# Two feature blocks of a feed-forward layer in ordinary products, on negated token quarters

## The chip, the cores and the metric

The kernel runs on one core of a Trainium2 chip. The metric is the time of the execution on the device in microseconds, the median of several runs: 866.68 us before the change.

## What is computed

One decoder layer on 544 tokens (512 prompt tokens and 32 sample tokens), of width 1024. A token mixer with three branches and an output projection comes first, then a layer norm, a SwiGLU feed-forward part with 2816 inner features, and a second layer norm. Only the seam between the first norm and the feed-forward part matters here:

```python
xp = _layernorm(ALPHA * xp + mp, ln1_g[l], ln1_b[l])
xp = _layernorm(ALPHA * xp + _ffn(xp, ffn_w_gate[l], ffn_w_up[l], ffn_w_down[l]), ln2_g[l], ln2_b[l])
...
def _ffn(x, wg, wu, wd):
    return (jax.nn.silu(x @ wg) * (x @ wu)) @ wd
```

## The kernel before

All matrix products are float32 products made of three passes: each operand is split into a high and a low part in float32r (`hi_lo`: ScalarE copies the high part, VectorE subtracts it to get the low part), and `gemm` (line 220) issues for every 128 rows of the contraction the matmuls high by high, high by low, low by high. Line 228 is the matmul of nearly all of them.

**The seam.** The output projection (`proj`) makes eight slices of 128 channels for two token halves, 288 and 256 tokens. ScalarE copies each result out of PSUM (`mo`, line 867), TensorE transposes it to tokens (line 819), VectorE adds the residual (line 878). `normalize` forms the norm, and `features` transposes the rows back (line 896) and writes the normalised tensor `xf` by channels with ScalarE (line 897). `xf` is 8 slices of 128 channels by 544 tokens.

**The feed-forward part.** The 2816 features are 22 blocks of 128, taken in two chunks of 11 (`NFC`). For a block, gate and up are one product of a 2x2 matrix of weight quarters (gate and up by two halves of the 1024 channels) with a 2x2 matrix of token quarters: `A11`, `A12` are the two channel halves of the first 272 tokens (`TH`), `A21`, `A22` those of the other 272. The kernel makes it with seven products in place of eight (Strassen's scheme in Winograd's form): `do(1, f)` to `do(7, f)`, each 12 matmuls of 272 columns. Their token operands `S[1]` to `S[7]` are made once: `S[1]` is -A11, `S[2]` is A12, `S[4]` is -A22, and 5, 6, 3, 7 are differences of quarters (`less`, line 1028) in the tiles `s1` to `s4` of the pool `sx`. Each is split by `operand` in two halves of its four channel slices. The weight operands are made per block: `prep_gate(f)` splits the two gate quarters, which serve products 1 and 2, and `prep_sums(f)` forms sums of the quarters and splits them for products 5, 7, 6, 3 and 4. Raw weights come with `ffn_load` into two buffers (`rawp`); split weights stand in a ring of three buffers (`wp`, tag `w`, shared with the projection's weights), one of two (`wpe`, tag `e`) and one of two (`t4`). The gate's and up's results are multiplied into `g`, which `put_g` splits into `gh` (ScalarE, line 977) and `gl` (GpSimd, line 978), the operands of the down projection.

Work is written in program order; a scheduler (the framework's own timeline) orders the instructions of each engine, and each engine then runs its queue in that order. At the seam the program writes:

```python
        operand(1, A11, True)
        operand(2, A12)
        do(1, 0)
        do(2, 0)
        prep_gate(1)
        do(1, 1)
        do(2, 1)
        less(s1, A21, A22)
        operand(5, s1)
        prep_sums(0)
```

so four products (48 matmuls) need only A11 and A12, and the fifth needs a difference of quarters, its split, and the sums of block 0's weights.

Of the kernel before, what the change touches and what calls it, by code (L numbers as in the profile page):

```python
# [16 lines left out]
P = 128  # L17
# [42 lines left out]
CNU = 0  # L60
KRB = 6
NFC = NF // 2
TH = T // 2
PSM = 5
W0C = ((0, 4), (4, 8))
# [83 lines left out]
def hybrid_layer_kernel(  # L149
# [747 lines left out]
            nc.scalar.activation(xf[:, kt, c0:c1], tp[:, :c1 - c0], AF.Identity, bias=vcol(V_B1 + kt), scale=vcol(V_G1 + kt))  # L897


    raws, gops, tops = {}, {}, {}  # L900

    def ffn_load(f):
        r = rawp.tile([P, 2048], F32, tag="raw", name=f"rawf{f}").rearrange("p (a c) -> p a c", a=4)
# [11 lines left out]
    def blocks(t, a):  # L915
        return [x[:, 512 * a:512 * a + 512].rearrange("p (k c) -> p k c", c=P) for x in t]

    def prep_gate(f):
        t = pair_of(wp, "w", 1024)
        hi_lo(t[0], t[1], raws[f][:, 0:2].rearrange("p a c -> p (a c)"))  # L920
        gops[f] = (blocks(t, 0), blocks(t, 1))

    def prep_sums(f):
        r = raws[f]
# [19 lines left out]
    ffn_load(0)  # L944
    ffn_load(1)
    prep_gate(0)
    for m in range(4):
        proj(res[m], 4 + m, 0)
    normalize(0)
    kts = iter(range(KD))  # L950
    for m in range(4):
        proj(res[m], 4 + m, 1)
        features(0, [next(kts) for _ in range(FEAT[m])])
    normalize(1)
    features(0, kts)
    features(1, range(KD))
# [23 lines left out]
    def do(i, f):  # L980
        if i == 1:
            X[f] = bank()
            prod(X[f], 1, f, True)
            M[f] = tmp("m", 2)
            nc.scalar.copy(M[f], X[f][:, :TH])
        elif i == 5:
            Y[f] = bank()
            prod(Y[f], 5, f, True)
            Q5[f] = tmp("q5", 2)
            nc.scalar.copy(Q5[f], Y[f][:, :TH])  # L990
        elif i == 2:
            Z[f] = bank()
            prod(Z[f], 2, f, True)
            SG1[f] = tmp("sg1", 2)
            nc.vector.tensor_tensor(out=SG1[f], in0=Z[f][:, :TH], in1=M[f], op=ALU.subtract)
            lasts.append(nc.scalar.activation(SG1[f], SG1[f], AF.Silu))
        elif i == 6:
            prod(X[f], 6, f, False)
            U2[f] = tmp("u2")
            nc.scalar.copy(U2[f], X[f][:, :TH])  # L1000
        elif i == 3:
            prod(Y[f], 3, f, False)
            g = tmp("g1")
            nc.vector.tensor_tensor(out=g, in0=Y[f][:, :TH], in1=U2[f], op=ALU.add)
            nc.vector.tensor_tensor(out=g, in0=g, in1=SG1[f], op=ALU.mult)
            put_g(g, f, 0)
        elif i == 7:
            prod(X[f], 7, f, False)
            C22[f] = tmp("c22")
            nc.vector.tensor_tensor(out=C22[f], in0=X[f][:, :TH], in1=Q5[f], op=ALU.add)  # L1010
        else:
            prod(X[f], 4, f, False)
            g = tmp("sg2")
            lasts.append(nc.scalar.activation(g, X[f][:, :TH], AF.Silu, scale=-1.0))
            nc.vector.tensor_tensor(out=g, in0=g, in1=C22[f], op=ALU.mult)
            put_g(g, f, TH)

    def operand(i, src, neg=False):
        h, l = S[i]
        for k in (slice(0, 2), slice(2, 4)):  # L1020
            if neg:
                nc.scalar.mul(h[:, k], src[:, k], -1.0)
                nc.vector.scalar_tensor_tensor(out=l[:, k], in0=src[:, k], scalar=-1.0, in1=h[:, k].bitcast(F32), op0=ALU.mult, op1=ALU.subtract)
            else:
                hi_lo(h[:, k], l[:, k], src[:, k])

    def less(out, a, b):
        nc.vector.tensor_tensor(out=out, in0=a, in1=b, op=ALU.subtract)

    with pool("sx", side="right", reuse_waits="tile") as sx:  # L1030
        s1, s2, s3, s4 = (sx.tile([P, 4, TH], F32, name=f"sx{i}") for i in range(4))
        operand(1, A11, True)
        operand(2, A12)
        do(1, 0)
        do(2, 0)
        prep_gate(1)
        do(1, 1)
        do(2, 1)
        less(s1, A21, A22)
        operand(5, s1)  # L1040
        prep_sums(0)
        less(s2, A11, s1)
        operand(6, s2)
        less(s4, A12, s2)
        operand(3, s4)
        less(s3, A21, A11)
        operand(7, s3)
        operand(4, A22, True)
    gp = ctx.enter_context(pool("gp", side="right", reuse_waits="tile"))
    gh = gp.tile([P, NFC, T], F32R, name="gh")  # L1050
    gl = gp.tile([P, NFC, T], F32R, name="gl")
    G = (gh, gl)
    pieces = ((0, 6), (6, 5))
    wds = []
# [6 lines left out]

    def ffn_blocks(f0, f1, todo):
        for f in range(f0, f1):
            if f + 2 < f1 and f + 2 > 1:
                ffn_load(f + 2)
            if f + 1 < f1:
                if f + 1 not in gops:
                    prep_gate(f + 1)
            else:
                todo()  # L1070
            for i in (6, 3):
                do(i, f)
            if f + 1 < f1:
                prep_sums(f + 1)
            do(7, f)
            if f + 1 < f1:
                do(1, f + 1)
            do(4, f)
            if f + 1 < f1:
                do(5, f + 1)  # L1080
                do(2, f + 1)

    for i in (5, 6, 3, 7, 4):
        do(i, 0)
    prep_sums(1)
    do(5, 1)

    def warm(wd):
        wd.prepare(0)
        wd.prepare(1)  # L1090

    ffn_load(2)
    ffn_blocks(1, NFC, lambda: warm(wds[0]))
    for m in range(KD):
        pss = [bank(), bank()]
        for j, (k0, k) in enumerate(pieces):
# [193 lines left out]
```

## Time and profile before

| | us |
|---|---|
| Three runs | 865.34, 866.68, 867.08 |
| Median | 866.68 |
| The profiled execution | 872.77 |
| Its span | 871.0 |
| TensorE busy in it | 827.4 (95%) |
| TensorE weight loads busy | 779.1 (89%) |
| VectorE busy | 580.5 (67%) |
| ScalarE busy | 413.4 (47%) |
| GpSimd busy | 174.1 (20%) |

The profile is of one execution. TensorE is busy in nearly all of the span; where it isn't, or where its granted clock is half, the stretch has to be looked at by itself. The page cuts the span into 40 slices of 21.8 us; the slice with the lowest granted clock begins at 479 us. A row's bracket gives the idle time of the engine before it and what ended it.

### The profile page before, as it was taken

The page shows a single profiled execution, that of the slowest core. Times are in us where ns is not written, and L with a number is a line of the kernel's source. Part 1 is how long each engine was busy: PE and PEld are TensorE (multiplying, and loading weights), DVE is VectorE, ACT ScalarE, POOL GpSimd, SP SyncE. Part 2 cuts the span into 40 slices and gives each one's busy share as a digit, 9 for nine tenths or more (in the row PEclk, how much of TensorE's full clock was granted, in tenths as well). Part 3 has the DMA queues.
Part 4 walks back from the last instruction along what each step waited for, and adds up shares of the span by engine and source line. Part 5 has one row for each costly group of instructions (what it writes and reads, how often), then busy time and mean ns, then how long its engine had stood idle before and what let it go on. Part 6 is the DMA issues. An engine that isn't in the chain of part 4 may idle for free.

```text
span 871.0 us, 16214 instructions
## 1 busy us (share of the span) xinstructions
PE 827.4 (95%) x6683; PEld 779.1 (89%) x6683; DVE 580.5 (67%) x968; ACT 413.4 (47%) x711; POOL 174.1 (20%) x198
## 2 busy tenths in 40 slices
PE   8998899999999998999998699999999999999992
PEld 7998799888898786789997699999999999999992
DVE  4899956888555544469455999883337888843436
ACT  5334368677654324344316556553124555543231
POOL 1430000002547766210000032211000111110002
PEclk9999899999999998999999699999999999999997
DMA  9413132412738987673500153322225333312222
GB/s 297 125 48 106 55 93 62 147 40 87 266 119 289 341 320 259 216 272 116 146 2 1 48 145 99 97 68 82 85 83 146 98 98 100 108 55 83 74 93 103
DMA packets 119401, 110.35 MB, mean 127 GB/s; under 512 B 4896, under 2 KB 111232, under 8 KB 117152
## 3 DMA queue, kind: packets, MB, share of 16 engines
q1 hardware_dynamic: 110848, 73.12, 28.2%
q0 software_dynamic: 8480, 36.20, 11.9%
q8 instruction: 52, 0.85, 0.4%
q14 instruction: 21, 0.17, 0.1%
HBM read 104.44 MB, written 4.87 MB: 125 GB/s over the span
## 4 chain that ended last, share of the span: by engine, by line
PE 81%; DVE 8%; DMA 5%; issue 2%; ACT 2%; POOL 1%; SPq 0%; DVEq 0%; POOLq 0%; ACTq 0%
PE mm L228 73%; DVE acc L436 3%; DMA raw<-in_w_in 2%; PE z L581 1%; PE o L607 1%; DVE wl L134 1%; PE tp L602 1%; PE z L677 1%; PE o L704 1%; PE tp L819 1%; DMA vr<-in_cv,piv 1%; DMA kr<-in_ck,pix 1%; DMA xt<-in_x_t 1%; ACT wh L133 0%; ACT xf L897 0%
## 5 line engine op out<-in xcount | busy, mean ns | idle before, releaser
L228 PE MATMUL mm<-xh,wh 128*128 128x256 f32 (+1 forms) x672 | 198.3, 295 | 3.0 <-DVE gt L492 0.9
L228 PE MATMUL mm<-xl,wh 128*128 128x256 f32 (+1 forms) x672 | 196.8, 293 | 0.5 <-DVE xl L215 0.4
L228 PE MATMUL mm<-xh,wl 128*128 128x288 f32 (+1 forms) x672 | 196.4, 293 | 0.4 <-DVE wl L134 0.4
L133 ACT CAST wh<-raw 128x1024 fp32r<-128x1024 f32 (+2 forms) x93 | 84.8, 915 | 164.0 <-PE mm L228 142.8
L134 DVE TENSOR_TENSOR wl<-raw,wh 128x1024 fp32r<-128x1024 f32 (+2 forms) x93 | 100.1, 1079 | 71.5 <-ACT wh L133 70.9
L228 PEld LDWEIGHTS mm<-xh,wh 128*128 128x128 f32 x672 | 128.0, 191 | 9.2 <-issue 3.8
L228 PEld LDWEIGHTS mm<-xl,wh 128*128 128x128 f32 x672 | 127.8, 190 | 4.5 <-issue 3.1
L228 PEld LDWEIGHTS mm<-xh,wl 128*128 128x128 f32 x672 | 127.8, 191 | 3.5 <-issue 2.4
L228 PE MATMUL mm<-gh,wh 128*128 128x288 f32 (+1 forms) x352 | 101.6, 290 | 0.0
L228 PE MATMUL mm<-gh,wl 128*128 128x288 f32 (+1 forms) x352 | 101.3, 288 | 0.0
L228 PE MATMUL mm<-gl,wh 128*128 128x288 f32 (+1 forms) x352 | 100.8, 287 | 0.0
L644 POOL DMA_INDIRECT kr<-in_ck,pix x64 | 67.0, 1047 | 36.1 <-issue 14.8
L228 PEld LDWEIGHTS mm<-gl,wh 128*128 128x128 f32 x352 | 66.4, 189 | 0.0
L228 PEld LDWEIGHTS mm<-gh,wl 128*128 128x128 f32 x352 | 66.2, 188 | 0.0
L228 PEld LDWEIGHTS mm<-gh,wh 128*128 128x128 f32 x352 | 65.9, 188 | 0.1
L978 POOL TENSOR_TENSOR gl<-g,gh 128x272 fp32r<-128x272 f32 x22 | 26.2, 1193 | 194.1 <-ACT gh L977 191.7
L978 POOL TENSOR_TENSOR gl<-sg,gh 128x272 fp32r<-128x272 f32 x22 | 19.7, 894 | 140.3 <-ACT gh L977 140.3
L436 DVE SCALAR_TENSOR_TENSOR acc<-ge,vt,acc 128x512 f32<-128x512 f32 x60 | 42.6, 752 | 0.1
L228 PE MATMUL mm<-mh,wh 128*128 128x256 f32 (+1 forms) x128 | 37.7, 294 | 0.0
L228 PE MATMUL mm<-ml,wh 128*128 128x256 f32 (+1 forms) x128 | 37.5, 293 | 0.0
L228 PE MATMUL mm<-mh,wl 128*128 128x256 f32 (+1 forms) x128 | 37.1, 290 | 0.0
L913 DVE TENSOR_TENSOR wl<-rawf,wh 128x1024 fp32r<-128x1024 f32 x22 | 28.3, 1287 | 8.8 <-ACT wh L912 8.7
(292 smaller groups left out, 2170.7 us busy)
## 6 DMA issues: line engine op xcount, KB each, us to landing
raw<-in_w_in SPq DMA_DIRECT2D x14, 1024.0 KB, 6.3
rawf<-in_w_g SPq DMA_DIRECT2D x22, 512.0 KB, 4.1
rawf<-in_w_u SPq DMA_DIRECT2D x22, 512.0 KB, 5.4
raw<-in_w_in SPq DMA_DIRECT2D x12, 512.0 KB, 3.8
raw<-in_w_d SPq DMA_DIRECT2D x16, 384.0 KB, 3.4
raw<-in_w_d SPq DMA_DIRECT2D x16, 320.0 KB, 3.2
raw<-in_w_out SPq DMA_DIRECT2D x4, 1024.0 KB, 5.4
raw<-in_w_att_o SPq DMA_DIRECT2D x4, 512.0 KB, 3.7
```

The lines of the kernel that those rows point to most:

```text
L133: self.nc.scalar.copy(hi[:, a:b], v[:, a:b])
L134: self.nc.vector.tensor_tensor(out=lo[:, a:b], in0=v[:, a:b], in1=hi[:, a:b].bitcast(F32), op=ALU.subtract)
L228: ins = nc.tensor.matmul(ps[:, :n], lw, rr, start=first and s == 0, stop=last and s == len(steps) - 1, **kw)
L436: nc.vector.scalar_tensor_tensor(out=o, in0=v, scalar=dw, in1=o, op0=ALU.mult, op1=ALU.add)
L581: nc.tensor.matmul(zps[s][:, :wd], a[r, qs], b[r, :wd], start=n_ == 0, stop=n_ == 2)
L602: nc.tensor.transpose(tp[:, kb], rc[:, s, kb * P:(kb + 1) * P], ident)
L607: nc.tensor.matmul(op_[64 * s:64 * s + 64, :P], vtok[:, kb, 64 * s:64 * s + 64], ats[s][:, kb], start=kb == 0, stop=kb == i)
L644: nc.gpsimd.indirect_dma_start(out=kr[:, u].rearrange("p h c -> p (h c)"), out_offset=None, in_=ck, in_offset=bass.IndirectOffsetOnAxis(ap ...
L677: behind["z"] = nc.tensor.matmul(zp[32 * jj:32 * jj + 32, :256], qbd[:, hp, b], kvt[b, "k", jj][:, :, hp], start=hp == 0, stop=hp == 3)
L704: nc.tensor.matmul(op_[32 * c:32 * c + 32], at[:, j], kvt[b, "v", j // 4][:, j % 4], start=j >= 4, stop=False)
L913: nc.vector.tensor_tensor(out=l, in0=src, in1=h.bitcast(F32), op=ALU.subtract)
L978: nc.gpsimd.tensor_tensor(out=gl[:, f % NFC, c0:c0 + TH], in0=g, in1=gh[:, f % NFC, c0:c0 + TH].bitcast(F32), op=ALU.subtract)
```

## The change

The first two blocks (`NPLAIN = 2`) are no longer made by seven products but by ordinary ones: `plain(f, hf)` makes gate and up of one block for one token half, with four times 12 matmuls into two PSUM banks. Its token operands are the four quarters, all negated: `S[1]` = -A11, `S[2]` = -A12, and -A21 and -A22, which stand in the tiles of `S[3]` and `S[4]`. `S[4]` is that operand anyway; `S[3]` gets its own contents later, after the plain products. The signs are taken back in the SiLU (`scale=-1.0`) and in the multiplication. The up quarters of these blocks are split by the new `prep_up` during the projection, and the loads of blocks 2 and 3 are issued there too.

The remaining nine blocks of the chunk, from `fs = 2` on, go by seven products. The differences are made by `of_dif` in two small tiles, one for each half of the channel slices, which are overwritten in place for operands 5, 6 and 3; operand 7's differences are made in a third buffer (that of `t13`), and its low part is subtracted on GpSimd. The pool `sx` is gone.

```diff
@@ -919,6 +920,11 @@
+    def prep_up(f):
+        t = pair_of(wpe, "e", 1024)
+        hi_lo(t[0], t[1], raws[f][:, 2:4].rearrange("p a c -> p (a c)"))
+        uops[f] = (blocks(t, 0), blocks(t, 1))
@@ -944,6 +950,8 @@
     prep_gate(0)
+    prep_up(0)
+    ffn_load(2)
@@ -951,6 +959,10 @@
         features(0, [next(kts) for _ in range(FEAT[m])])
+        if m == 1:
+            prep_gate(1)
+            prep_up(1)
+            ffn_load(3)
@@ -992,8 +1004,8 @@
-            nc.vector.tensor_tensor(out=SG1[f], in0=Z[f][:, :TH], in1=M[f], op=ALU.subtract)
-            lasts.append(nc.scalar.activation(SG1[f], SG1[f], AF.Silu))
+            nc.vector.tensor_tensor(out=SG1[f], in0=Z[f][:, :TH], in1=M[f], op=ALU.add)
+            lasts.append(nc.scalar.activation(SG1[f], SG1[f], AF.Silu, scale=-1.0))
@@ -1022,33 +1034,59 @@
-    with pool("sx", side="right", reuse_waits="tile") as sx:
-        s1, s2, s3, s4 = (sx.tile([P, 4, TH], F32, name=f"sx{i}") for i in range(4))
-        operand(1, A11, True)
-        operand(2, A12)
-        do(1, 0)
-        do(2, 0)
-        prep_gate(1)
-        do(1, 1)
-        do(2, 1)
-        less(s1, A21, A22)
-        operand(5, s1)
-        prep_sums(0)
-        less(s2, A11, s1)
-        operand(6, s2)
-        less(s4, A12, s2)
-        operand(3, s4)
-        less(s3, A21, A11)
-        operand(7, s3)
-        operand(4, A22, True)
+    def plain(f, hf):
+        ps = [bank(), bank()]
+        sg = tmp("sg1", 2)
+        for j, ops in enumerate((gops[f], uops[f])):
+            for i in range(2):
+                gemm(ps[j], ops[i], S[((1, 2), (3, 4))[hf][i]], [0, 1, 2, 3], 0, TH, first=i == 0, last=i == 1)
+            if j == 0:
+                lasts.append(nc.scalar.activation(sg, ps[0][:, :TH], AF.Silu, scale=-1.0))
+        nc.vector.scalar_tensor_tensor(out=sg, in0=ps[1][:, :TH], scalar=-1.0, in1=sg, op0=ALU.mult, op1=ALU.mult)
+        put_g(sg, f, hf * TH)
+
+    KH = (slice(0, 2), slice(2, 4))
+    dif = [s7.tile([P, 2, TH], F32, tag="dif", bufs=2, name=f"dif{k}") for k in range(2)]
+
+    def of_dif(i, a, b):
+        for d, k in zip(dif, KH):
+            less(d, a[:, k], d if b is None else b[:, k])
+        for d, k in zip(dif, KH):
+            hi_lo(S[i][0][:, k], S[i][1][:, k], d)
+
+    fs = NPLAIN
+    operand(1, A11, True)
+    operand(2, A12, True)
+    plain(0, 0)
+    operand(3, A21, True)
+    operand(4, A22, True)
+    plain(1, 0)
+    plain(0, 1)
+    plain(1, 1)
+    of_dif(5, A21, A22)
+    prep_gate(fs)
+    do(1, fs)
+    do(2, fs)
+    prep_sums(fs)
+    do(5, fs)
+    of_dif(6, A11, None)
+    for k in KH:
+        d = s7.tile([P, 2, 512], F32, tag="t13", bufs=1, name="d7")[:, :, :TH]
+        less(d, A21[:, k], A11[:, k])
+        nc.scalar.copy(S[7][0][:, k], d)
+        nc.gpsimd.tensor_tensor(out=S[7][1][:, k], in0=d, in1=S[7][0][:, k].bitcast(F32), op=ALU.subtract)
+    prep_gate(fs + 1)
+    of_dif(3, A12, None)
@@ -1080,17 +1118,21 @@
-    for i in (5, 6, 3, 7, 4):
-        do(i, 0)
-    prep_sums(1)
-    do(5, 1)
+    do(6, fs)
+    do(7, fs)
+    do(1, fs + 1)
+    do(2, fs + 1)
+    do(3, fs)
+    do(4, fs)
+    prep_sums(fs + 1)
+    do(5, fs + 1)
...
-    ffn_load(2)
-    ffn_blocks(1, NFC, lambda: warm(wds[0]))
+    ffn_load(fs + 2)
+    ffn_blocks(fs + 1, NFC, lambda: warm(wds[0]))
```

What this does to the queues stands at three places.

TensorE, behind the last transposes of `xf`. A row is line, operation, output<-token operand, weight operand; `mm` is a PSUM bank, `wh`/`wl` split gate quarters or sums, `eh`/`el` split up quarters. Before:

```order
L228 MATMUL mm_5555<-s2h_5475,wh_5536 128x272
L896 MATMUL tp_5459<-et_80,y_4471 128x128 x2
L228 MATMUL mm_5555<-s2l_5476,wh_5536 128x272
L896 MATMUL tp_5463<-et_80,y_4471 128x128 x2
L228 MATMUL mm_5555<-s2h_5475,wl_5537 128x272
L228 MATMUL mm_5617<-s5h_5477,wh_5578 128x272
L228 MATMUL mm_5617<-s5l_5478,wh_5578 128x272
```

After:

```order
L229 MATMUL mm_5524<-s2h_5493,el_5089 128x272
L229 MATMUL mm_5524<-s2h_5493,eh_5088 128x272
L897 MATMUL tp_5481<-et_80,y_4471 128x128 x2
L229 MATMUL mm_5524<-s2l_5494,eh_5088 128x272
L229 MATMUL mm_5524<-s2h_5493,el_5089 128x272
L229 MATMUL mm_5524<-s2h_5493,eh_5088 128x272
L229 MATMUL mm_5524<-s2l_5494,eh_5088 128x272
```

Before, the last transposes and product 2 are followed at once by product 5. After, they stand inside the first plain product, and product 5 (`s5h`) is row 3343 of the queue, 163 rows below the last one shown. Up to the last projection matmul and the first six transposes of the second token half, TensorE's queue is the same in both.

VectorE, from the second half's normalisation on (`sx`, `dif` differences of quarters; `t` the first sum of a block's weights; `sg` the SiLU tile). Before:

```order
L1023 SCALAR_TENSOR_TENSOR s1l<-xf,s1h 128x544 x2
L913 TENSOR_TENSOR s2l<-xf,s2h 128x544 x2
L1028 TENSOR_TENSOR sx_5495<-xf 128x1088
L1023 SCALAR_TENSOR_TENSOR s4l<-xf,s4h 128x544
L913 TENSOR_TENSOR s7l<-sx_5495,s7h 128x544 x2
L926 TENSOR_TENSOR t_5576<-rawf_5078 128x1024
L1028 TENSOR_TENSOR sx_5493<-xf 128x1088
L995 TENSOR_TENSOR sg_5533<-mm,m 128x272
L995 TENSOR_TENSOR sg_5568<-mm,m 128x272
L1023 SCALAR_TENSOR_TENSOR s4l<-xf,s4h 128x544
L929 TENSOR_TENSOR rawf_5078<-t_5576,rawf_5078 128x512
L913 TENSOR_TENSOR wl<-t_5576,wh 128x1024
```

After:

```order
L1035 SCALAR_TENSOR_TENSOR s1l<-xf,s1h 128x544 x2
L1035 SCALAR_TENSOR_TENSOR s2l<-xf,s2h 128x544 x2
L1035 SCALAR_TENSOR_TENSOR s3l<-xf,s3h 128x544 x2
L1035 SCALAR_TENSOR_TENSOR s4l<-xf,s4h 128x544
L1041 TENSOR_TENSOR dif_5513<-xf 128x544
L932 TENSOR_TENSOR t_5792<-rawf_5092 128x1024
L1041 TENSOR_TENSOR dif_5514<-xf 128x544
L1055 SCALAR_TENSOR_TENSOR sg_5525<-mm,sg_5525 128x272
L1035 SCALAR_TENSOR_TENSOR s4l<-xf,s4h 128x544
L935 TENSOR_TENSOR rawf_5092<-t_5792,rawf_5092 128x512
L914 TENSOR_TENSOR s5l<-dif_5513,s5h 128x544
L914 TENSOR_TENSOR s5l<-dif_5514,s5h 128x544
```

The low parts of all four negated quarters now stand ahead of the differences, and each difference is two instructions of 544 columns in place of one of 1088; the sums are those of block 2 (`rawf_5092`), not of block 0.

GpSimd, behind the last `memset` of the norm (`gl` the low part of a block's result). Before:

```order
L978 TENSOR_TENSOR gl<-g_5658,gh 128x272
L978 TENSOR_TENSOR gl<-sg_5689,gh 128x272
L978 TENSOR_TENSOR gl<-g_5761,gh 128x272
L978 TENSOR_TENSOR gl<-g_5892,gh 128x272
L978 TENSOR_TENSOR gl<-sg_5823,gh 128x272
```

After:

```order
L990 TENSOR_TENSOR gl<-sg_5525,gh 128x272
L990 TENSOR_TENSOR gl<-sg_5588,gh 128x272
L990 TENSOR_TENSOR gl<-sg_5643,gh 128x272
L1087 TENSOR_TENSOR s7l<-d_5829,s7h 128x544
L1087 TENSOR_TENSOR s7l<-d_5833,s7h 128x544
L990 TENSOR_TENSOR gl<-sg_5698,gh 128x272
L990 TENSOR_TENSOR gl<-g_5918,gh 128x272
```

The four plain results come first, and operand 7's two low parts stand among them.

On ScalarE the casts of the two up quarters and of block 2's gate quarters (`eh`, `eh`, `wh<-rawf_5092`) stand between the projection's copies; the order of SyncE's loads is the same as before: those of blocks 2 and 3 stand directly behind those of blocks 0 and 1, and each waits for its raw buffer to be read out.

## Rows read from the trace of the kernel before

**Rows 1.** The page: span, TensorE, and the granted clock in 40 slices.

```profile
span 871.0 us, 16214 instructions
...
PE 827.4 (95%) x6683; PEld 779.1 (89%) x6683; DVE 580.5 (67%) x968; ACT 413.4 (47%) x711; POOL 174.1 (20%) x198
...
PEclk9999899999999998999999699999999999999997
```

**Rows 2.** Windows (us; engine busy us, (x) instructions, clock, DMA share, GB/s) around the gap.

```profile
468.38:496.55 28.17, 19.05 (x99) 17.70 (x98) 24.21 (x31) 18.25 (x33) 0.00 (x0) 0.70 0.12 33
496.55:598.60 102.05, 102.05 (x813) 102.05 (x812) 85.31 (x116) 58.40 (x107) 24.17 (x20) 1.00 0.36 98
```

**Rows 3.** TensorE timeline (start, length, engine, line, operation, [idle <- releaser]), 468 to 599 us.

```profile
468.38 0.39 PE L228 MATMUL mm<-s1h,wh 128*128 128x272 f32 x1
469.14 0.60 PE L228 MATMUL mm<-s1l,wh 128*128 128x272 f32 x1 [0.36 <-DVE s1l L1023]
469.53 0.43 PE L228 MATMUL mm<-s1h,wl 128*128 128x272 f32 x1
...
472.25 0.39 PE L228 MATMUL mm<-s1h,wh 128*128 128x272 f32 x1
...
473.63 0.82 PE L896 MATMUL tp<-et,y 128*128 128x128 f32 x6
474.20 0.37 PE L228 MATMUL mm<-s2l,wh 128*128 128x272 f32 x1
...
481.31 0.39 PE L228 MATMUL mm<-s5h,wh 128*128 128x272 f32 x1 [3.42 <-ACT s5h L912]
485.54 0.59 PE L228 MATMUL mm<-s5l,wh 128*128 128x272 f32 x1 [3.84 <-DVE s5l L913]
...
490.13 0.60 PE L228 MATMUL mm<-s5h,wh 128*128 128x272 f32 x1 [1.50 <-ACT wh L912]
...
496.55 0.29 PE L228 MATMUL mm<-s7h,wh 128*128 128x272 f32 x1
...
598.94 0.30 PE L228 MATMUL mm<-gh,wh 128*128 128x288 f32 x1
```

**Rows 4.** Chain that ended last (start us, us, what), 479 to 486 us.

```profile
479.30 1.28 DVE sx L1028
...
483.66 1.11 issue
484.77 0.73 DVE s5l L913
```

**Rows 5.** Windows of one us each: TensorE's granted clock is the PEclk column.

```profile
469.50:470.50 1.00, 1.00 (x6) 1.00 (x6) 1.00 (x3) 1.00 (x3) 0.00 (x0) 0.50 0.00 0
472.50:473.50 1.00, 1.00 (x10) 1.00 (x9) 0.00 (x0) 0.00 (x0) 0.00 (x0) 1.00 0.00 0
494.50:495.50 1.00, 1.00 (x6) 1.00 (x6) 1.00 (x2) 0.00 (x0) 0.00 (x0) 0.50 1.16 340
```

**Rows 6.** Timelines of VectorE and GpSimd, then GpSimd's groups by line: single durations.

```profile
468.36 1.36 DVE L1023 SCALAR_TENSOR_TENSOR s1l<-xf,s1h 128x544 fp32r<-128x544 f32 x2 [0.61 <-ACT s1h L1022]
...
478.16 1.22 DVE L926 TENSOR_TENSOR t<-rawf 128x1024 f32<-128x1024 f32 x1
...
500.25 0.43 DVE L1004 TENSOR_TENSOR g<-mm,u 128x272 f32<-128x272 f32 x1
...
503.18 2.30 POOL L978 TENSOR_TENSOR gl<-g,gh 128x272 fp32r<-128x272 f32 x1 [91.50 <-ACT gh L977]
...
L750 POOL TENSOR_TENSOR mg<-mg,gt 128x544 f32<-128x544 f32 x8 | 10.8, 1360 | 26.9 <-DVE gt L749 26.8
```

**Rows 7.** Projection stage, 427 to 438 us: windows, then timelines of ScalarE and TensorE.

```profile
428.00:434.00 6.00, 6.00 (x51) 5.99 (x49) 2.23 (x4) 1.33 (x3) 0.00 (x0) 1.00 0.00 0
...
427.61 1.05 ACT L912 CAST wh<-rawf 128x1024 fp32r<-128x1024 f32 x1 [2.83 <-PE mm L228]
...
434.37 0.37 ACT L867 COPY mo<-mm 128x256 f32<-128x256 f32 x1 [3.00 <-PE mm L228]
...
437.31 0.71 PE L819 MATMUL tp<-et,mo 128*128 128x128 f32 x5
```

More of the change, by code (lines that the diff above doesn't have):

```diff
@@ L62 @@
 NFC = NF // 2
+NPLAIN = 2
 TH = T // 2
@@ L897, in features @@
             nc.scalar.activation(xf[:, kt, c0:c1], tp[:, :c1 - c0], AF.Identity, bias=vcol(V_B1 + kt), scale=vcol(V_G1 + kt))
-    raws, gops, tops = {}, {}, {}
+    raws, gops, uops, tops = {}, {}, {}, {}
     def ffn_load(f):
@@ L1024, in operand @@
             else:
-                hi_lo(h[:, k], l[:, k], src[:, k])
+                nc.scalar.copy(h[:, k], src[:, k])
+                nc.vector.tensor_tensor(out=l[:, k], in0=src[:, k], in1=h[:, k].bitcast(F32), op=ALU.subtract)
     def less(out, a, b):
         nc.vector.tensor_tensor(out=out, in0=a, in1=b, op=ALU.subtract)
-    with pool("sx", side="right", reuse_waits="tile") as sx:
-        s1, s2, s3, s4 = (sx.tile([P, 4, TH], F32, name=f"sx{i}") for i in range(4))
-        operand(1, A11, True)
-        operand(2, A12)
-        do(1, 0)
-        do(2, 0)
-        prep_gate(1)
-        do(1, 1)
-        do(2, 1)
-        less(s1, A21, A22)
-        operand(5, s1)
-        prep_sums(0)
-        less(s2, A11, s1)
-        operand(6, s2)
-        less(s4, A12, s2)
-        operand(3, s4)
-        less(s3, A21, A11)
-        operand(7, s3)
-        operand(4, A22, True)
     gp = ctx.enter_context(pool("gp", side="right", reuse_waits="tile"))
@@ L1063, in ffn_blocks @@
         for f in range(f0, f1):
-            if f + 2 < f1 and f + 2 > 1:
+            if f + 2 < f1:
                 ffn_load(f + 2)
```

## Prediction, before the changed kernel was run

> **What bounds the kernel now.** I read the page first, then windows around the worst slice, TensorE's timeline there, and the chain. TensorE is busy 827.4 us of a span of 871.0 [rows 1], so time can come only from stretches where it idles or runs at half clock, or from fewer matmuls. The clock's string has one deep dip, the slice at 479 us [rows 1]. The reader is to see in the windows that the seam between norm and feed-forward, 468.38 to 496.55 us, takes 28.17 us, with TensorE busy for 19.05 of them at a mean granted clock of 0.70, while the next 102 us are full at 1.00 [rows 2]. In the timeline two long waits (3.42 and 3.84 us) end with the first matmuls of product 5: at 481.31 for the operand's high part, at 485.54 for its low part, with 1.50 us more at 490.13 for the sums of the weights [rows 3]. The chain shows what is late: VectorE's difference of quarters at 479.30, another step of its queue, then the low part at 484.77 [rows 4]; it is busy 24.21 of the 28.17 us [rows 2]. So the seam is bound by VectorE (and ScalarE) making operands, and TensorE pays twice, by waiting and by a granted clock that is 0.50 of 2.4 GHz (1.2 GHz) after the waits, still at 494.50 [rows 5].
>
> **What the seam loses.** From 496.55 to the first down-projection matmul at 598.94 lie 102.39 us [rows 3] and 813 matmuls [rows 2]: 0.126 us each at full clock. At half clock twelve steps from 469.53 to 472.25 take 2.72 us [rows 3], 0.227 each, so a matmul at half clock costs 0.101 more. Six transposes take 0.57 us (473.63 to 474.20) [rows 3]. The seam holds 87 matmuls and 10 transposes (the window's 99 counts two that straddle its edges): 87 x 0.126 + 10 x 0.095 = 11.9 us at full clock. It takes 28.17, so 16.2 us are lost: 9.1 idle (28.17 - 19.05), 7.1 to the clock.
>
> **The change, part by part.** Sum against the profiled execution.
>
> 1. *More matmuls: +3.0 us.* Two blocks go from 7 x 12 = 84 matmuls each to 96, two plain calls of 48: 24 more, x 0.126. All are on the path, since TensorE is.
>
> 2. *The waits of product 5 and the second clock drop: -16.2 us, less what stays.* Behind the last transposes TensorE now has 192 plain matmuls and 24 of products 1 and 2 of block 2 before product 5. They need only the negated quarters. -A11 is there as before (its low part ended TensorE's wait at 469.14 [rows 3]); the others are copies and subtractions without a difference ahead of them. By the order shown, VectorE does the four low parts first: two instructions take 1.36 us [rows 6], 0.68 each. TensorE reaches -A21 after 96 matmuls, at about 484 us; ScalarE's and VectorE's queues, added up with these durations from the last `xf` writes at 478.5, have -A21 by 477 and all of -A22 by 481. So I expect no wait in the plain stretch.
>
> 3. *The first clock drop stays: +1.8 us.* The transposes ahead of 468.38 and the wait inside them are the same, so the clock should again be 0.50 at 469.5 and 1.00 at 472.5 [rows 5]. From 468.38 to 472.3 that is 17.5 matmuls, x 0.101 = 1.8. Bounds: 0, if TensorE's closer work from 468.4 keeps the clock up; and 4.7, if it behaves as in the second drop, where it is 0.50 from 485.54 to past 494.50 [rows 3, 5] and 10.7 us would hold 47 matmuls. I take 1.8, from the nearer drop. The Trainium skill, page "TensorE: Matmul & The Clock Gate", Part 1, says that the point of release varies between runs of one kernel; no run here shows that yet, and by it the term would be anything between these bounds.
>
> 4. *Later deadlines.* Product 5 is reached at 468.4 + 1.8 + 1.0 + 216 x 0.126, about 498.4. Its operand and the first sums are, by the same adding up, split by 483 and 490. VectorE has also less to do: block 0's and block 1's sums (a first sum of 1.22 us [rows 6], and their splits) are gone. From 468.4 to block 4's gate split it has some 30 us of instructions, and TensorE wants that split only near 511. Cost 0 under this cover; without it, up to one wait like those of before, 3.84 us [rows 3].
>
> 5. *Operand 7 on GpSimd.* The low part of 544 columns took GpSimd 1.36 us alone, in the nearest group of the same shape [rows 6]; half that shape took 2.30 beside a busy VectorE [rows 6], so 1.4 to 4.6 each. The second buffer of differences waits for the first low part, and block 3's first sum for the second. In the worst case the second ends near 503; TensorE wants operand 7 near 505.5 and block 3's sums near 508. Cost 0; the margin is the thinnest of all. The Trainium skill, page "SBUF — State Buffer", section "Who interferes with whom", says that GpSimd and a VectorE instruction with two SBUF inputs exclude each other for a whole instruction; the 2.30 agrees. By that rule VectorE, too, is held for up to the two low parts; that speaks for the first rival.
>
> 6. *Plain results.* Four SiLUs and four multiplications from PSUM (0.43 us for such a read [rows 6]) free the banks; with five banks the first is wanted again only after 96 matmuls. Cost 0.
>
> 7. *The projection.* Two up splits, block 2's gate split and its load move there. VectorE has 2.23 and ScalarE 1.33 us of work in 6, and no DMA runs, from 428 to 434 [rows 7]. Block 2's cast waits for a buffer that the projection's fourth slice frees near 434.1, and stands ahead of the copy at 434.37: 1.05 us later [rows 7] it is done at 435.8, and TensorE's transposes of it come at 437.31 [rows 7]. Cost 0, margin 1.5 us.
>
> **Sum:** 3.0 - 16.2 + 1.8 = -11.4 us. The profiled execution took 872.77 us, 6.1 above the median; I take the same saving off both: 861.4 for it, 855.3 for the median 866.68. A measurement here can tell about 0.2% (1.7 us) from no change.
>
> **Rivals.**
>
> *A. The wait is moved, not removed.* VectorE, held by GpSimd, or ScalarE's queue is late at product 5, operand 7 or block 3's sums. For: VectorE was 86% busy in the seam (24.21 of 28.17), and the thin margins of 5. Against: the sums of two blocks are gone, and the deadlines lie 15 us later. Price: one wait of up to 3.84 us, and if the clock falls after it, 3 us more: 857 to 862.
>
> *B. The clock stays at 1.2 GHz in the plain stretch (slower).* Then each plain matmul costs 0.101 more. If all 192 do, that is 19.4 instead of 1.8: -11.4 + 17.6 = +6.2, 872.9. It decides from 1.8 / 0.101 + 11.4 / 0.101, about 131 slow matmuls. For: after the second drop the clock stayed at 0.50 past 494.5 [rows 5]. Against: it had a wait in it (490.13 [rows 3]), and the first drop ended while TensorE was fed without one.
>
> *C. The cost goes into the projection.* A late load or cast holds up block 2's gate split, and with it the copies behind it on ScalarE, and the norm. Price: from the margin of 1.5 us on, 1 to 3 us: 856 to 858. That the change doesn't do what it says is no case: the order shows 216 matmuls ahead of product 5.
>
> *D. The clock doesn't drop at all:* 1.8 us less, 853.5.
>
> **How the numbers follow.** Forecast 0.70 (854 to 857 with the runs' own spread), A 0.14, B 0.05, C 0.04, D 0.07. The likeliest gives 855.3. The range goes from D's 853.2 to 861.0, which takes in the upper bound of the clock (+2.9) and most of A; left out are B and A's end. Faster by over 0.2%: all but B and a waiting A of several pieces, 0.94; the same 0.02; slower 0.04.
>
> **What would show it.** In the profile after: some 24 more matmuls; TensorE without a wait from 469 to 511; the window 475 to 496 full at clock 1.00 where there is now the dip; the clock at 0.50 once, near 469 to 472; the first matmul on `gh` about 119 us after the first on `s1h`, where it is 130.56 now (598.94 - 468.38 [rows 3]). A row with a wait of over 1 us on `s5`, `s6`, `s7` or the first sums speaks for A; a clock of 0.50 beyond 476, for B; a later first `s1h`, for C. The forecast is wrong if the seam loses more than 6 us.

## The result, and the profile after

| | before | changed |
|---|---|---|
| Median of four runs each, us | 866.01 | 854.27 |
| Ratio, 95% interval | | 0.9876, 0.9848 to 0.9905 |
| The profiled execution, its span | 872.77, 871.0 | 858.24, 854.5 |

The changed kernel is faster by 11.7 us of the medians; 855.3 had been forecast, a gain of 11.4. The ratio also takes in a fifth run of the changed kernel (856.39) and stands for 1.2%, 10.7 us of 866, with an interval of 8.2 to 13.2.

The profiled executions differ by more than the medians, 16.5 us of span. The span is therefore cut at three marks that both traces have: the first projection matmul (408.30 before, 402.52 after), the first one on `s1h` (468.38, 462.82) and the first on `gh` (598.94 [rows 3], 582.45). Before the projection the changed kernel's execution is 5.78 us ahead, in code that the change doesn't touch; from there to `gh` it needs 179.93 us where it was 190.64, 10.71 less; the rest is 272.05 and 272.06. So 10.71 us belong to the change. The 5.78 us come from an earlier stage; ScalarE's timeline in the kernel before shows a late weight load there:

```profile
330.30 1.04 ACT L133 CAST wh<-raw 128x1024 fp32r<-128x1024 f32 x1 [12.28 <-DMA raw<-in_w_in]
```

Its window from 320 to 340 us (columns: us, then TensorE, weight loads, VectorE, ScalarE, GpSimd, clock, DMA share, GB/s):

```profile
320.00:340.00 20.00, 16.69 (x136) 14.87 (x139) 7.99 (x16) 6.21 (x8) 9.67 (x11) 0.83 0.85 309
```

The same window of the changed kernel is full:

```profile
320.00:340.00 20.00, 20.00 (x205) 15.84 (x203) 10.55 (x20) 8.16 (x9) 13.65 (x15) 1.00 0.96 349
```

How long the stages ahead of the projection take varies with the execution and the chip: in the control run below the changed kernel itself reaches its first projection matmul only at 426.03. On the chips of the experiments all kernels lie higher, the one before too (its medians there are 884 to 893 us), while the last 272 us are the same to 0.1 us in all fourteen profiles.

The page of the changed kernel, against [rows 1]: 24 matmuls more, and the deep dip of the clock is gone.

```profile
span 854.5 us, 16236 instructions
...
PE 824.3 (96%) x6707; PEld 778.4 (91%) x6707; DVE 570.0 (67%) x956; ACT 409.8 (48%) x703; POOL 175.8 (21%) x200
...
PEclk9999899999999999999998999999999999999997
```

Its windows, first over as long a stretch as [rows 2], then in pieces:

```profile
462.82:490.99 28.17, 28.17 (x210) 28.17 (x209) 21.89 (x31) 18.09 (x34) 6.85 (x4) 0.92 0.11 30
490.99:582.45 91.46, 91.46 (x728) 91.46 (x727) 74.26 (x101) 51.67 (x95) 18.76 (x18) 1.00 0.32 88
...
455.00:460.00 5.00, 4.77 (x30) 3.17 (x28) 2.43 (x10) 3.80 (x9) 0.00 (x0) 1.00 0.00 0
460.00:465.00 5.00, 3.60 (x15) 3.31 (x16) 4.29 (x9) 4.99 (x10) 0.00 (x0) 0.56 0.00 0
465.00:470.00 5.00, 5.00 (x33) 5.00 (x33) 0.94 (x2) 2.33 (x6) 0.00 (x0) 0.76 0.01 3
```

In 28.17 us TensorE was busy for 19.05 [rows 2]; now it is busy for all of it, with 210 instructions in place of 99. Only the head is slow: the granted clock is half (1.2 GHz) from within the wait for the norm until 467. TensorE's timeline (columns of [rows 3]):

```profile
461.40 1.77 PE L897 MATMUL tp<-et,y 128*128 128x128 f32 x6 [1.51 <-DVE y L889]
462.82 0.57 PE L229 MATMUL mm<-s1h,wh 128*128 128x272 f32 x1
...
467.05 0.43 PE L229 MATMUL mm<-s1h,wh 128*128 128x272 f32 x1
467.28 0.36 PE L229 MATMUL mm<-s1l,wh 128*128 128x272 f32 x1
467.47 0.29 PE L229 MATMUL mm<-s1h,wl 128*128 128x272 f32 x1
...
493.27 0.29 PE L229 MATMUL mm<-s5h,wh 128*128 128x272 f32 x1
...
500.33 0.29 PE L229 MATMUL mm<-s7h,wh 128*128 128x272 f32 x1
...
502.33 0.29 PE L229 MATMUL mm<-s5h,wh 128*128 128x272 f32 x1
...
582.45 0.29 PE L229 MATMUL mm<-gh,wh 128*128 128x288 f32 x1
```

Behind 461.40 no row up to `gh` has a wait. When the operands are ready stands on VectorE's timeline:

```profile
476.14 1.36 DVE L914 TENSOR_TENSOR s5l<-dif,s5h 128x544 fp32r<-128x544 f32 x2
...
482.96 1.21 DVE L914 TENSOR_TENSOR wl<-t,wh 128x1024 fp32r<-128x1024 f32 x1
...
493.14 1.78 DVE L932 TENSOR_TENSOR t<-rawf 128x1024 f32<-128x1024 f32 x1 [0.91 <-POOL s7l L1087]
...
496.52 1.22 DVE L914 TENSOR_TENSOR wl<-t,wh 128x1024 fp32r<-128x1024 f32 x1
```

and on GpSimd's:

```profile
476.47 2.90 POOL L990 TENSOR_TENSOR gl<-sg,gh 128x272 fp32r<-128x272 f32 x1 [70.57 <-ACT gh L989]
479.81 0.77 POOL L990 TENSOR_TENSOR gl<-sg,gh 128x272 fp32r<-128x272 f32 x1 [0.45 <-ACT gh L989]
...
491.37 1.74 POOL L1087 TENSOR_TENSOR s7l<-d,s7h 128x544 fp32r<-128x544 f32 x1 [2.48 <-ACT s7h L1086]
```

Product 5's operand is split at 477.5 and its weights at 484.2; it starts at 493.27: 9 us of margin. Operand 7 is there at 493.1 for 500.33, and block 3's sums at 497.7 for 502.33, the thinnest margin of these, 4.6 us. GpSimd holds VectorE up once, by 0.91 us, and nobody waits for that.

### The profile page after: what moved, and what is told of

Same layout as the page of the kernel before. It is cut to its first block, busy times and chain, and to the rows that moved or that the text cites. A ratio compares the mean times of both kernels' runs of the same rounds, so it can differ in the third digit from the quotient of the medians.

```text
span 854.5 us, 16236 instructions
## 1 busy us (share of the span) xinstructions
PE 824.3 (96%) x6707; PEld 778.4 (91%) x6707; DVE 570.0 (67%) x956; ACT 409.8 (48%) x703; POOL 175.8 (21%) x200
## 4 chain that ended last, share of the span: by engine, by line
PE 87%; DVE 7%; issue 2%; DMA 2%; ACT 1%; POOL 1%; SPq 0%; DVEq 0%; ACTq 0%
PE mm L229 77%; DVE acc L437 3%; PE z L678 2%; PE o L705 2%; PE z L582 1%; PE o L608 1%; PE tp L603 1%; DVE wl L135 1%; PE tp L820 1%; DMA vr<-in_cv,piv 1%; DMA xt<-in_x_t 1%; PE tp L897 0%; DVE mg L516 0%; DVE mg L500 0%; POOL mg L751 0%
## 5 line engine op out<-in xcount | busy, mean ns | idle before, releaser
L990 POOL TENSOR_TENSOR gl<-sg,gh 128x272 fp32r<-128x272 f32 x24 | 22.9, 956 | 209.5 <-ACT gh L989 209.5
L990 POOL TENSOR_TENSOR gl<-g,gh 128x272 fp32r<-128x272 f32 x20 | 21.3, 1066 | 110.2 <-ACT gh L989 107.8
```

The lines of the kernel that those rows point to most:

```text
L990: nc.gpsimd.tensor_tensor(out=gl[:, f % NFC, c0:c0 + TH], in0=g, in1=gh[:, f % NFC, c0:c0 + TH].bitcast(F32), op=ALU.subtract)
```

## The experiments

**Theory.** TensorE waited because four products (48 matmuls) were too little work to make operand 5 and its weights behind, and the clock fell in that wait. The plain blocks give 192 matmuls of cover; that is the gain, less 24 matmuls. **Rivals:** the quicker recipe of the operands (halves in place, operand 7 on GpSimd) is the gain; or the clock alone is; or VectorE, spared the sums of two blocks, makes the operands sooner.

Every run is compared with the kernel before on the same chip. Because an early stage varies between executions by more than the effects, the traces' stretches are given beside the ratio: S from the first matmul on `s1h` to the first on `gh`, P to it from the last projection transposes (`tp<-et,mo`), F to it from the first projection matmul; "slow" counts the rows of 0.42 us or more among the first matmuls, which stand at half clock.

| kernel | ratio, 95% interval | S, us | P, us | F, us | slow |
|---|---|---|---|---|---|
| before | 1 | 130.56 | 136.27 | 190.64 | 13 |
| changed | 0.9876, 0.9848 to 0.9905 | 119.63 | 125.56 | 179.93 | 19 |
| changed again (e12) | 0.9884, 0.9835 to 0.9933 | 119.11 | 124.83 | 179.20 | 15 |
| operands alone (e2) | 1.0001, 0.9972 to 1.0030 | 130.50 | 136.21 | 190.59 | 12 |
| halves alone (e13) | 0.9970, 0.9945 to 0.9995 | 128.39 | 134.33 | 188.70 | 9 |
| plain blocks alone (e3) | 0.9883, 0.9841 to 0.9926 | 119.25 | 124.97 | 179.33 | 13 |
| one block (e1) | 0.9899, 0.9867 to 0.9931 | 121.12 | 127.06 | 181.43 | 7 |
| one block, operand 7 on VectorE (e8) | 0.9868, 0.9831 to 0.9904 | 121.77 | 127.49 | 181.86 | 13 |
| three blocks (e5) | 0.9903, 0.9871 to 0.9936 | 120.40 | 126.24 | 180.61 | 11 |
| before, wait filled (e7) | 0.9986, 0.9964 to 1.0007 | 130.29 | 136.00 | 190.37 | 12 |
| changed, filled ahead of the wait (e4) | 0.9874, 0.9830 to 0.9919 | 119.75 | 125.69 | 181.26 | 20 |
| changed, wait filled (e6) | 0.9858, 0.9822 to 0.9894 | 117.87 | 123.58 | 177.95 | 0 |
| early products (e9) | 0.9824, 0.9781 to 0.9866 | | 122.79 | 177.35 | 0 |
| early products, pinned (e11) | 0.9827, 0.9785 to 0.9868 | | 122.40 | 176.77 | 0 |

**The control (e12).** The changed kernel, unaltered.

> The changed kernel as it is, on the chip of the experiments. Theory: what differs between chips and executions lies ahead of the change, so the stretch from the first product to the down-projection is 119.3 to 120.4 us as in its first profile (119.63) and in the runs with two plain blocks, with some 12 to 20 of the first matmuls at half clock; the ratio to the kernel before 0.986 to 0.990. Rival (the waits come back where the engines are timed a little otherwise): 122 or more.

S is 119.11, 0.2 below the theory's range, with 15 slow matmuls in place of 19: 4 x 0.101 = 0.4 of the 0.5 us between the two. So S less 0.101 for each slow matmul is 117.6 to 117.7 in both, and that number can be compared between runs to a few tenths.

**Does the recipe of the operands carry the gain? (e2, e13, e3)** First the recipe without plain blocks, in the kernel before:

```diff
-        less(s1, A21, A22)
-        operand(5, s1)
-        prep_sums(0)
-        less(s2, A11, s1)
-        operand(6, s2)
...
+    of_dif(5, A21, A22)
+    prep_sums(0)
+    of_dif(6, A11, None)
...
+        nc.gpsimd.tensor_tensor(out=S[7][1][:, k], in0=d, in1=S[7][0][:, k].bitcast(F32), op=ALU.subtract)
```

> Edit: the kernel before, all blocks in seven products, with the change's differences alone (by K halves, in place; the low part of operand 7 on GpSimd). Theory: product 5 is still reached after 48 matmuls, so TensorE still waits for operand 5 and the clock still falls a second time; the first half difference ends 0.7 us sooner than a whole one, so at most 1 to 5 of the 9.1 us of waits go: 861 to 866. Rival (the quicker operands are the gain): 853 to 857.

No gain. TensorE's waits, where [rows 3] had 3.42, 3.84 and 1.50 us:

```profile
490.84 0.39 PE L228 MATMUL mm<-s5h,wh 128*128 128x272 f32 x1 [3.24 <-ACT wh L912]
491.71 0.39 PE L228 MATMUL mm<-s5l,wh 128*128 128x272 f32 x1 [0.48 <-DVE s5l L913]
492.85 0.59 PE L228 MATMUL mm<-s5h,wl 128*128 128x272 f32 x1 [0.74 <-DVE wl L913]
498.37 0.60 PE L228 MATMUL mm<-s6l,eh 128*128 128x272 f32 x1 [2.37 <-DVE s6l L913]
502.88 0.60 PE L228 MATMUL mm<-s3l,eh 128*128 128x272 f32 x1 [1.43 <-DVE s3l L913]
```

Product 5's waits shrink from 7.3 to 4.5 us, and operands 6 and 3 wait 3.8 in their place, with the clock still at half behind the last of them (0.60 us for the matmul at 502.88). One of the delays was GpSimd's, a `s7l` of 3.60 us that VectorE waited for, so the same was run with operand 7 on VectorE:

> Edit: the kernel before with the change's differences by halves in place, and the low part of operand 7 left on VectorE. The run with the operands alone took 130.50 us from the first product to the down-projection, as the kernel before does (130.56), but there the third GpSimd instruction, 3.60 us, held up a difference on VectorE before operand 3. Theory (VectorE's and ScalarE's work cannot be done in the 48 matmuls ahead of product 5, in whatever order): TensorE's waits move among operands 5, 6 and 3 and the clock falls a second time, 128.5 to 131 us. Rival (the halves are worth 4 us or more and GpSimd hid it): 126.5 or less.

S is 128.39, 0.1 below the theory's range: the halves by themselves are worth 2.2 us (0.4 of it four slow matmuls less), and with operand 7 on GpSimd they are gone again. This is one profile each, and part of it is the clock behind the waits: by the granted clocks of windows of 5 us it was half for 10.2 us in this run's second drop and for 13.6 in e2's. The rest needs the plain blocks, which the opposite run shows, the changed kernel with neither halves nor GpSimd:

```diff
-        for d, k in zip(dif, KH):
-            less(d, a[:, k], d if b is None else b[:, k])
+        less(dif, a, dif if b is None else b)
...
-        nc.gpsimd.tensor_tensor(out=S[7][1][:, k], ...
+        nc.vector.tensor_tensor(out=S[7][1][:, k], ...
```

> Edit: the changed kernel with whole differences of 1088 columns and the low part of operand 7 on VectorE. Theory: both are hidden behind the plain blocks, which leave operand 5 some 20 us and operands 6, 7 and 3 over 5 us of margin: 854.3, within 1 us of the changed kernel. Rival (the halves and GpSimd keep operand 7 or 3 off the path): a wait of 3 us or more before operand 6, 7 or 3, 857 or more.

S less the slow matmuls is 119.25 - 1.3 = 117.9, within 0.3 us of the changed kernel, and no row has a wait. Under the plain blocks' cover the recipe is worth nothing that S shows.

**Does VectorE make the operands sooner?** The profiles before and after settle the third rival. VectorE's timeline in the kernel before:

```profile
482.43 1.22 DVE L913 TENSOR_TENSOR wl<-t,wh 128x1024 fp32r<-128x1024 f32 x1
...
484.77 1.35 DVE L913 TENSOR_TENSOR s5l<-sx,s5h 128x544 fp32r<-128x544 f32 x2
```

Counted from the first product, operand 5 is split after 17.7 us before and 14.7 after, the first sums after 15.3 before and 21.4 after: the pair is complete 3.6 us later than before. What moved is the time at which TensorE asks for it, 9.5 us before (481.31 less the wait of 3.42) and 30.5 after. What the spared sums do for the operands behind product 5 no run here parts from the cover.

**Is it the clock alone? (e7)** The wait of the kernel before was filled with matmuls whose result nobody reads.

```diff
         do(2, 1)
+        spare = auxb()
+        for i in range(56):
+            ins = nc.tensor.matmul(spare[:, :TH], gops[1][0][0][:, i % 4], S[2][0][:, i % 4], start=i == 0, stop=i == 55)
```

> Edit: the kernel before with 56 matmuls of 272 columns, whose result nobody reads, between product 2 of block 1 and product 5 of block 0, where TensorE waits 7.3 us for operand 5: the clock part alone, with no cover over VectorE's and ScalarE's work. Theory: the clock no longer falls before product 5, yet operands and weights come no sooner; only the stretch from 490.1 to 496.6 us that ran at half clock with no wait becomes shorter, 3.2 us: 127.3 us from the first product to the down-projection where the kernel before has 130.5. Rival 1 (the clock is most of the gain): 123 or less. Rival 2 (the wait for the next weights grows and the clock falls there): 130.

S is 130.29: the second rival; my theory missed by 3 us. The timeline:

```profile
487.63 7.16 PE L1041 MATMUL tp<-s2h,wh 128*128 128x272 f32 x56
495.44 0.39 PE L228 MATMUL mm<-s5l,wh 128*128 128x272 f32 x1 [0.52 <-DVE s5l L913]
500.02 0.59 PE L228 MATMUL mm<-s5h,wh 128*128 128x272 f32 x1 [2.82 <-ACT wh L912]
```

and the windows:

```profile
487.00:494.00 7.00, 7.00 (x58) 7.00 (x57) 7.00 (x10) 6.18 (x12) 0.00 (x0) 1.00 0.00 0
494.00:500.00 6.00, 2.68 (x20) 2.24 (x18) 6.00 (x7) 3.21 (x5) 0.00 (x0) 0.94 0.00 0
500.00:506.00 6.00, 5.98 (x24) 5.57 (x25) 6.00 (x10) 2.62 (x4) 0.00 (x0) 0.50 0.47 132
```

The clock holds through the filler and product 5 runs at full speed, but its successor's weights come no sooner: the wait for them grows from 1.50 to 2.82 us, and the clock falls there. VectorE is busy in every microsecond of these 19, so it is the bound there; holding the clock ahead of it gave 0.3 us.

**How much cover is needed? (e1, e8, e5)** One plain block in place of two (`NPLAIN = 1`, without block 1's two `plain` calls and its preparation in the projection):

> Edit: one plain block in place of two. Theory (the gain is 192 plain matmuls of cover over the making of operand 5 and its weights): 12 matmuls fewer give 1.5 us back, but product 5 is reached some 12 us sooner, near 480.5 on the clock of the changed kernel's profile, where operand 5 was there at 477.5 and the weights' sums only at 484.2; so TensorE waits 0 to 3.7 us again, on those weights first: 853 to 856.5 us where the kernel before takes 866. Rival 1 (quicker operands are the gain, the cover counts for nothing): no wait, 852.8. Rival 2 (all of the cover is needed): waits of 6 us and a second clock drop, 860 or more.

By S the time fell into the theory's range (1.5 us over the changed kernel's 119.63); the ratio alone puts it at 857.3 on the first chip's scale (854.5 to 860.1), a little above. And the late operand is another than I named: the first product 5 no longer waits; operands 6 and 3 do, and the next product 5 waits 0.44 us for its weights.

```profile
505.44 0.40 PE L229 MATMUL mm<-s6l,eh 128*128 128x272 f32 x1 [0.19 <-DVE s6l L914]
507.38 0.39 PE L229 MATMUL mm<-s3h,eh 128*128 128x272 f32 x1 [1.05 <-ACT s3h L913]
510.91 0.40 PE L229 MATMUL mm<-s3l,eh 128*128 128x272 f32 x1 [0.71 <-DVE s3l L914]
517.30 0.39 PE L229 MATMUL mm<-s5h,wh 128*128 128x272 f32 x1 [0.44 <-ACT wh L913]
```

The window around them:

```profile
500.00:520.00 20.00, 17.56 (x128) 16.20 (x127) 20.00 (x27) 11.77 (x22) 8.35 (x5) 1.00 0.20 55
```

The bracketed waits add up to 2.4 us, but 128 matmuls start where a full 20 us hold 159 (20 / 0.126): some 3.9 us are lost. S less the slow matmuls is 121.12 - 0.7 = 120.4, 2.8 above two blocks although it has 12 matmuls less. GpSimd's part was tried with operand 7 on VectorE:

> Edit: one plain block, and the low part of operand 7 on VectorE in place of GpSimd. The one-block run waited 2.4 us in all for operands 6 and 3 and a weight cast, and its stretch from the first product to the down-projection was 121.2 us, 1.5 over the changed kernel in spite of 12 matmuls fewer. Theory (VectorE, busy without a gap from 488 to 514 there, is the limit, and GpSimd's 7.7 and 1.8 us instructions slow it): near 120 to 121, between the one-block run and the 118.2 that no wait would give. Rival 1 (GpSimd does relieve VectorE): 122 or more. Rival 2 (GpSimd alone was the brake): 118.5 or less.

S less the slow matmuls is 121.77 - 1.3 = 120.5, the same as with GpSimd (the raw 121.77 lies between the theory and the first rival; the slow matmuls account for it). VectorE is busy for all 20 us from 500 to 520 in this run, too, and TensorE starts 131 matmuls: who subtracts operand 7 makes no difference that these two profiles show. Three blocks:

> Edit: three plain blocks in place of two. Theory: two blocks leave no wait, so a third adds only its 12 matmuls, 12 x 0.126 = 1.5 us over the changed kernel: the stretch from the first product's first matmul to the down-projection's first one becomes 121.2 us (119.7 with two blocks, 130.5 before). Rival (margins of operands 6, 7 and 3 still cost something with two blocks): 119 us or less. Rival 2 (the third block's own weights come late): over 122.

No wait, and S less the slow matmuls is 120.40 - 1.1 = 119.3, 1.6 above two blocks, for 12 matmuls forecast at 1.5 (the raw 120.40 lies between the theory's 121.2 and the rival's 119). So two blocks are the best of the three: one leaves waits that cost more than it saves, three buy nothing. The stretches say so; the ratios of the runs with plain blocks overlap and don't.

**The clock drop that stays (e4, e6).** Twelve useless matmuls of 256 columns were to fill the wait for the norm.

> Edit: the changed kernel with 12 more matmuls of 256 columns, whose result nobody reads, on TensorE's queue between the last projections' transposes and those that wait for the second normalization (1.51 us of wait). Theory: they fit into the wait (12 x 0.11 = 1.3 us) and the clock no longer falls before the plain blocks, which saves the 20 matmuls at half clock, 2.5 us: 851.8 to 852.5. Rival 1: the clock falls all the same, since what runs before is thin too: 854 to 855. Rival 2: the 12 matmuls delay the transposes: 855 to 856.

They ran at 472.02, ahead of the wait and not in it (it is still there, 1.51 us before 478.41), cost their 1.3 us in F, and the clock fell as before, with 20 slow matmuls. The run says nothing on a filled wait; the next one pins them behind the last transposes (`features` now returns its last one):

```diff
+NFILL = 12
...
+    ins = features(0, kts)
+    spare = bank()
+    with tc.issue_after(ins.ins):
+        for i in range(NFILL):
+            nc.tensor.matmul(spare[:, :256], res[3][0][:, 0], mh[:, i % KD, :256], start=i == 0, stop=i == NFILL - 1)
     features(1, range(KD))
```

> Edit: the changed kernel with 12 matmuls of 256 columns, whose result nobody reads, fixed on TensorE's queue behind the last transposes before the second normalization's wait, so that they run in that wait (in the filled-wait run before they ran ahead of it, and the clock fell all the same). Theory: they take 1.3 of the 1.51 us, the clock holds, and the 6.6 us at half clock (1.0 of them idle) become 2.8 us shorter: 117 us from the first product to the down-projection where the changed kernel has 119.7, and the six transposes 0.9 us shorter ahead of it. Rival: the clock falls all the same, 119.7 and no gain.

TensorE's timeline:

```profile
478.06 1.68 PE L974 MATMUL mm<-mh,wh 128*128 128x256 f32 x12
479.63 0.51 PE L899 MATMUL tp<-et,y 128*128 128x128 f32 x2
480.30 0.65 PE L899 MATMUL tp<-et,y 128*128 128x128 f32 x4 [0.16 <-ACT xf L900]
480.84 0.39 PE L230 MATMUL mm<-s1h,wh 128*128 128x272 f32 x1
```

The windows:

```profile
475.00:480.00 5.00, 4.88 (x32) 3.64 (x31) 3.18 (x11) 4.61 (x9) 0.00 (x0) 1.00 0.00 0
480.00:485.00 5.00, 4.84 (x36) 4.37 (x36) 3.47 (x6) 4.34 (x9) 0.00 (x0) 1.00 0.02 3
```

The clock doesn't fall in this stretch. S is 117.87, 1.8 less than in the changed kernel's first profile, 1.2 less than in the control. 2.7 had been expected, but that counted the half clock ahead of the first product as well; the 19 slow matmuls alone are 1.9.

**A version with a still shorter stretch (e9, e11).** In place of useless matmuls the wait can take useful ones: the high part of operand 1 needs only the first half's `xf`, and eight products of its first two K tiles need no low part.

```diff
+    nc.scalar.mul(s1h[:, 0:2], xf[:, 0:2, :TH], -1.0)
     normalize(1)
-    features(0, kts)
+    ins = features(0, kts)
+    pse = [bank(), bank()]
+    with tc.issue_after(ins.ins):
+        for j, ops in enumerate((gops[0], uops[0])):
+            for k in range(2):
+                for a in range(2):
+                    nc.tensor.matmul(pse[j][:, :TH], ops[0][a][:, k], s1h[:, k], start=k == 0 and a == 0, stop=False, skip_group_check=True)
...
```

The first plain product then leaves out these eight. In e11 the second half of operand 1's high part is also held back behind the norm's square root on ScalarE.

> Edit: the changed kernel with the high part of operand 1 made before the second normalization, and the eight products of its first two K tiles that need no low part (gate and up, high and low weights) put into that normalization's wait on TensorE in place of useless matmuls. Theory: they keep the clock as the useless ones did, and 8 x 0.126 = 1.0 us of work leaves the stretch behind: from the last projection transposes to the down-projection 122.3 to 123.2 us, where the wait filled with useless matmuls had 123.58 and the changed kernel 125.56. Rival 1: ScalarE makes the second half of the operand ahead of the square root of the norm and delays the wait's end by up to 0.6 us: 123.2 to 124. Rival 2: eight or ten matmuls are too few to hold the clock: 125 or more.

> Edit: the early products, with the second half of operand 1's high part held behind the norm's square root on ScalarE. Theory: the norm is not delayed, but two more products stand ahead of the last transposes on TensorE and wait for that half behind ScalarE's 1.28 us table load: 122.5 to 123.5 us from the last projection transposes to the down-projection. Rival: the gap in TensorE's work before those two products is enough for the clock to fall: 125 or more.

TensorE's timeline in e9:

```profile
488.65 0.29 PE L229 MATMUL mm<-s1h,wh 128*128 128x272 f32 x1
488.78 0.29 PE L229 MATMUL mm<-s1h,eh 128*128 128x272 f32 x1
489.62 0.50 PE L899 MATMUL tp<-et,y 128*128 128x128 f32 x2 [0.55 <-DVE y L890]
490.27 0.66 PE L899 MATMUL tp<-et,y 128*128 128x128 f32 x4 [0.15 <-ACT xf L900]
```

In e9 the scheduler adds two more matmuls, ten in all, the wait shrinks to 0.55 us and the clock holds. P is 122.79, as expected; in e11 it is 122.40, 0.1 below the theory's range. F is 1.9 to 3.2 us shorter than the changed kernel's. The medians on one chip say the same, 877.53 and 876.83 against 880.46 for the changed kernel there, but the intervals of the ratios overlap: the stretch is shown to be shorter, the whole time probably so.

## Why the prediction was right

- *Matmuls, +3.0.* 24 more, as counted; the third block measures 1.6 for 12, 3.2 for 24.
- *Waits and second clock drop, -16.2.* Both are gone. What is left of the sum (S fell by 10.93) is -10.93 - 3.0 - 1.9 = -15.8. The split of the 16.2 into 9.1 of idling and 7.1 of clock was off, though: 49 matmul rows of the seam are at half clock, 49 x 0.101 = 4.9 us, and the other 2 us are busy time too, such as that of the first matmul behind a wait, which takes 0.39 to 0.60 us [rows 3].
- *The first clock drop stays, +1.8.* It stays, 19 slow matmuls (1.9 us), 15 in the other run. Its place was wrong: the prediction had it fall behind the first product, as before at 469; it fell in the wait ahead of it (mean 0.56 from 460 to 465), so the six transposes ran slowly as well, and P fell by 10.71, 0.2 less than S. The full clock came back 4.5 us behind the first product (467.28) in this profile and 3.5 us behind it in the control. The Trainium skill, page "TensorE: Matmul & The Clock Gate", Part 1, says the point of release varies between runs of one kernel. The two profiles, with 19 and 15 slow matmuls, agree.
- *Deadlines.* Counted from the first product, operand 5 was expected at 14.6, the first sums at 21.6, product 5 at 30.0 us; they came at 14.7, 21.4 and 30.5.
- *Operand 7 on GpSimd.* 1.36 and 1.74 us, at the low end of 1.4 to 4.6; ready at 30.3 where 34.6 was the worst case. The thinnest of the margins reckoned with is indeed that of block 3's sums (4.6 us).
- *Plain results and the projection.* From the first projection matmul to the last projection transposes it is 54.37 us before and after; block 2's cast stands at 428.42, 25.9 us behind the first projection matmul, where 25.8 was worked out.
- *The median.* The whole saving was taken off the median; the profiled pair differs by 5.78 us more, in the early stage. That the medians came within 0.3 us of the forecast 11.4 is partly luck: the stretch that the sum is about, F, is 10.7 us shorter in this pair of profiles and 11.4 in the control, the ratio stands for 10.7 (8.2 to 13.2), and the stages ahead of the projection vary by more than the difference.

Of the rivals, A (a moved wait) is what the operands alone do, and what one block does; B and C are not seen in any profile. D, no clock drop, needed a filled wait.

One argument was too simple, though its sum held: idling and clock were treated as two losses. The filled kernel before shows that the second can't be had without the first: there the clock held in the filled waits, fell in the next one, and S was shorter by only 0.3 us.

## What to carry to other kernels

When TensorE waits for another engine that is itself busy, look for TensorE work whose operands already exist and put it in the wait; even a costlier form of work that has to be done anyway can pay, up to the point where the waits are gone (here two blocks, not one or three, by the stretches). Keeping the clock up in a wait gave next to nothing here where the engine waited for was the bound (0.3 us), and 1.2 to 2.0 us of P where a short wait stood ahead of work that was all ready. Cut the span at marks that both traces share before comparing profiles: the stage that was changed repeats to some tenths of a us, the whole program doesn't.

## What the runs showed of the hardware

GpSimd's subtraction of one shape (`gl`, 128x272) took 0.77 us in the changed kernel at 479.81, 2.90 at 476.47, and in the one-block run 7.68, while VectorE worked without a gap. Nor was VectorE free of it beside the 0.77: its `t4l` of 128x512 at 479.87 took 1.26 us, where one takes 0.69 at 499.92. The one-block run:

```profile
494.13 7.68 POOL L986 TENSOR_TENSOR gl<-sg,gh 128x272 fp32r<-128x272 f32 x1 [69.14 <-ACT gh L985]
501.78 1.82 POOL L1081 TENSOR_TENSOR s7l<-d,s7h 128x544 fp32r<-128x544 f32 x1
```

and VectorE's timeline in the same run:

```profile
502.64 2.74 DVE L914 TENSOR_TENSOR s6l<-dif,s6h 128x544 fp32r<-128x544 f32 x2
```

The two low parts on VectorE at 502.64 took 2.74 us beside GpSimd's 1.82 and a `gl` of 1.25 us behind it, where the pair takes 1.36 elsewhere (476.14 of the changed kernel). The prediction's upper bound for GpSimd, 4.6 us for twice that shape, was too low. The Trainium skill, page "SBUF — State Buffer", section "Who interferes with whom", lets either engine block for a whole instruction of the other. The 2.74 agrees. The 7.68 us are longer than any single VectorE instruction here, so by that rule GpSimd would have waited for several in a row, which no run here takes apart.

A wait of TensorE isn't at once a fall of its clock. In the kernel before the granted clock stayed at 1.00 (2.4 GHz) through the whole wait of 3.42 us, and it fell only within the next wait, the 3.84 us ahead of 485.54 (0.86 on average from 482 to 483, 0.50 from 483 to 485.5):

```profile
477.90:481.30 3.40, 0.00 (x0) 0.00 (x0) 3.40 (x6) 3.31 (x8) 0.00 (x0) 1.00 0.00 0
```

It also held through waits of up to 1.05 us in the one-block run, but fell within the 1.51 us wait for the norm in the changed kernel. In the control, with the same wait up to 484.90, it was still full for the transposes and fell at the first product (0.63 on average from 486 to 487):

```profile
485.00:486.00 1.00, 0.85 (x6) 0.57 (x6) 0.48 (x1) 1.00 (x4) 0.00 (x0) 1.00 0.00 0
```

So the length of a single wait doesn't tell here whether the clock falls, and nothing in these runs tells what does.
